# A hybrid layer on one core: four row tiles of S5's input as block products, with the first half of K split over two passes

## The chip, the core and the metric

One core of a Trainium2 chip runs one launch that computes one layer. The metric is device time in microseconds (us); less is better. The engines are called by the profile's names: PE (matrix products), DVE and ACT (element-wise work on rows of 128 partitions), POOL (element-wise work, and the queue that issues most DMAs here), SP (a queue that only issues DMAs).

## The reference, cut to what matters

The layer takes 1032 tokens: 1024 of a prompt and one for each of eight decode streams. The width is 2048.

```
h = rmsnorm(x, g_pre)
q, k, v, za, ub, zb, ga, gb = split(h @ w_in)      # 80 row tiles of 128 columns
ya = groupnorm(retention(q, k, v)) * silu(za)
yb = glu(gelu(s5(ub))) ; yb = yb * silu(zb)
y  = sigmoid(ga) * (ya @ w_pa) + sigmoid(gb) * (yb @ w_pb)
out = x + rmsnorm(y @ w_out, g_post)
```

`ub` is the input of S5, 1024 columns of `w_in`: row tiles 32 to 39 of the transposed product. S5 is a linear recurrence over tokens for each group of 16 columns, so it needs all eight tiles before it can begin. The states of both recurrences are outputs too.

## The kernel before, in words

**Number form.** Everything is float32. A product of float32 matrices is made of three matmuls on split operands: high weight by high input, high weight by low input, low weight by high input. The high part is a cast by ACT (`hi`, tiles `whia`, `whib`, `whic` in turn), the low part is the remainder that DVE subtracts (`lo`, tiles `wloa`, `wlob`, `wloc`). Weights come from memory as quarters of a row tile (128 x 512) and are split on the core; three pairs of buffers go round.

**Two ways to make a row tile of h @ w_in.** In the linear way (`linear`, L255, matmuls in `three`, L227 to L229), a row tile is four quarters of K, each with three thirds of the tokens (384, 384 and 264 columns), 16 k-tiles in all. In the other way, a pair of row tiles and half of K make a *step*: the blocks are multiplied by Winograd's form of Strassen's rule, seven products of 24 matmuls each (`product`, L923, its matmuls L935) in place of eight. The seven input operands of a half of K are 28 *form tiles* (128 x 516): sums and differences of blocks of the normed input. They are built once (`build_forms`, L767), written to the memory array `fm_d`, and later loaded, split and kept on the core. A pair is visited twice, once for each half of K. In the first visit the four results of a step are written to `pt_d` (L984); in the second they are read from it with an accumulating DMA (L986) into the tile with the new results, and go on to what the pair is for (`result`, from L978).

**The order of the work.** (1) In the start block, 16 k-tiles of `x` are loaded, scaled by `g_pre`, split, and squared for the norm, and row tiles 32 and 33 are made on the way. (2) Row tile 34 is made by `linear`; meanwhile `rms_bcast` (L278) turns the sums of squares into `rstd`, the inverse root for each token, and spreads it over 128 partitions by eight small matmuls with a diagonal matrix (L306) and one for the last 8 tokens. (3) Row tiles 35 to 39 are made by `linear` (L802, L803). Meanwhile `build_forms` makes all 56 form tiles: eight groups, each of two loads of `x` (`fx`, POOL's queue, L774), two scalings on DVE (L783), four sums or differences on DVE (`fo`, L85) and seven writes on ACT's queue (L793). (4) Two row tiles of v (16 and 17) are made by the linear way; `first_forms` meanwhile loads and splits the 28 form tiles of the first half of K. (5) 70 steps follow: 35 pairs with the first half, then 35 pairs with the second. Between the two, from two steps before the end of the first pass on, the 28 tiles on the core are replaced one by one (the *exchange*). S5 runs behind the first pass, from step 1 (`s5_params`) and step 4 (`s5_all`) on; retention behind the second. (6) Steps of the same kind for the later matrices, and the last norm.

**What sets the order.** Row tiles 32 to 39 are evacuated by `evac_ub`: DVE multiplies by `rstd` and permutes the tokens into a tile `ubp` (128 x 8 x 144: 8 runs of 128 tokens, with 8 columns of neighbours or zeros on both sides), one DMA writes it to `ub_d`, and S5 reads `U` from there. Side work is a list of generators `bg`. `slot()` (L172) advances the first of them by one `yield`; `linear` calls it once per quarter, a step once per product. What a product leaves to do later goes into `at(g, f)`, with g counted in products: `late_work(g)` runs it, and `LAG = 4` is the usual distance. Each engine works its instructions in the order in which they were written, and so does each DMA queue issue. Before a weight quarter is used, `prep` or `wtile` puts its cast into ACT's order and its remainder into DVE's, two quarters or products ahead of the matmuls.

S5 first sets the borders of a memory array `t_d` to zero: 16 times a POOL `MEMSET` of the tile `a` (L568) and a POOL DMA of it (L569). All helpers that add, subtract or multiply record their instruction at L85.

## Time and profile before

| what | value |
|---|---|
| time, median of 3 runs | 2532.88 us (2532.5 to 2534.38) |
| the profiled execution: its own time | 2534.5 us |
| its span, first to last instruction | 2532.6 us |
| instructions | 52483 |
| TensorE clock granted, mean of the span | 0.998 of full speed |
| moved by DMA | 519.10 MB, 205 GB/s in the mean |
| of it issued by POOL's queue (software) | 301.75 MB |
| third row tile of ub | 53.7 to 81.2 us |
| fourth to eighth row tile | 81.2 to 193.9 us |
| two row tiles of v | 193.9 to 239.5 us |
| 70 steps | from 239.5 us on |

The span is what the profile shows; the execution's own time is 1.9 us longer. The page gives for each engine the busy time and its share of the span; a PE that is busy can still be the bound only where nothing else ends last, which is what the chain of waits tells: it starts at the last instruction and goes back to what released it, again and again. The idle time in front of a group of instructions stands behind its busy time, with an arrow to what ended it. "x4" is the number of instructions in a group. L-numbers are those of the kernel before.

### The profile page before, as it was taken

Reading aid. Unit: us, or ns where it says so; the run is one execution under the profiler, and the core shown is the slowest. Engines: PE = TensorE matmul, PEld = TensorE weight load, DVE = VectorE, ACT = ScalarE, POOL = GpSimd, SP = SyncE. Lnnn points to the kernel's source line nnn. Section 1 sums busy time; section 2 is a strip of 40 time slices with the busy share of each in tenths; the row PEclk is TensorE's granted clock in tenths of the full one; section 3 lists DMA queues with packets and bytes.
Section 4 is the critical chain, followed back from the end, with each engine's and each line's share of the span. In section 5 each row is a group of like instructions: output and inputs, shape, how many; then the busy total and the mean of one; then the engine's idle time right before and its main releaser. Section 6 shows DMA issues by size and latency. Waiting matters only on the chain.

```text
span 2532.6 us, 52483 instructions
## 1 busy us (share of the span) xinstructions
PE 2508.4 (99%) x19948; PEld 2463.6 (97%) x19948; DVE 1975.9 (78%) x4149; ACT 965.4 (38%) x1731; POOL 763.4 (30%) x1276
## 2 busy tenths in 40 slices
PE   9999999999999999999999999999999999999998
PEld 8999999999999999999999999999999999999976
DVE  7655998898898877557986767667897878989784
ACT  7013223333333335343334444445552422455532
POOL 0103222322322222332334444434332222433320
PEclk9999999999999999999999999999999999999999
DMA  6886434444434437888879888888888689857884
GB/s 198 258 266 218 155 126 133 130 126 137 132 126 129 129 122 252 203 218 200 209 195 248 228 226 229 211 224 243 275 288 282 228 243 314 289 189 167 218 299 136
DMA packets 233755, 519.10 MB, mean 205 GB/s; under 512 B 34224, under 2 KB 61312, under 8 KB 232736
## 3 DMA queue, kind: packets, MB, share of 16 engines
q0 software_dynamic: 103008, 301.75, 41.7%
q1 hardware_dynamic: 91552, 159.30, 20.3%
q10 hardware_dynamic: 38944, 54.71, 6.8%
q8 instruction: 157, 2.57, 0.4%
q14 instruction: 94, 0.77, 0.1%
HBM read 342.37 MB, written 173.25 MB: 204 GB/s over the span
## 4 chain that ended last, share of the span: by engine, by line
PE 91%; issue 4%; DVE 2%; POOL 1%; DMA 1%; ACT 0%; POOLq 0%; DVEq 0%; SPq 0%; ACTq 0%
PE acc L935 71%; PE acc L1763 4%; PE mm L229 3%; PE mm L228 3%; PE mm L227 3%; DMA a<-mg_d 1%; DVE a L85 1%; PE misc L729 1%; PE misc L728 1%; PE misc L1134 1%; PE misc L1144 1%; PE misc L1113 1%; POOL zr L1582 1%; PE misc L679 1%; PE misc L1146 0%
## 5 line engine op out<-in xcount | busy, mean ns | idle before, releaser
L935 PE MATMUL acc<-a,whic 128*128 128x256 f32 (+1 forms) x3664 | 606.1, 284 | 1.4 <-ACT whib L916 0.6
L935 PE MATMUL acc<-a,whib 128*128 128x256 f32 (+1 forms) x3656 | 604.7, 284 | 2.5 <-DVE u L85 2.4
L935 PE MATMUL acc<-a,whia 128*128 128x256 f32 (+1 forms) x3656 | 604.7, 284 | 1.8 <-ACT whic L916 0.9
L935 PEld LDWEIGHTS acc<-a,whib 128*128 128x128 f32 x3656 | 504.4, 188 | 7.3 <-ACT whia L916 2.6
L935 PEld LDWEIGHTS acc<-a,whic 128*128 128x128 f32 x3664 | 506.2, 188 | 3.5 <-issue 1.0
L935 PEld LDWEIGHTS acc<-a,whia 128*128 128x128 f32 x3656 | 504.9, 188 | 3.9 <-issue 1.7
L935 PE MATMUL acc<-a,wloc 128*128 128x256 f32 (+2 forms) x1832 | 382.2, 283 | 0.4 <-DVE wloc L85 0.4
L935 PE MATMUL acc<-a,wlob 128*128 128x256 f32 (+2 forms) x1828 | 381.2, 283 | 0.0
L935 PE MATMUL acc<-a,wloa 128*128 128x256 f32 (+2 forms) x1828 | 381.0, 283 | 0.0
L935 PEld LDWEIGHTS acc<-a,wloc 128*128 128x128 f32 x1832 | 286.8, 188 | 1.2 <-DVE wloc L85 1.2
L935 PEld LDWEIGHTS acc<-a,wlob 128*128 128x128 f32 x1828 | 286.3, 188 | 0.2
L935 PEld LDWEIGHTS acc<-a,wloa 128*128 128x128 f32 x1828 | 286.3, 188 | 0.0
L916 ACT CAST whia<-wraw 128x512 fp32r<-128x512 f32 x142 | 88.4, 623 | 223.5 <-PE acc L935 170.4
L916 ACT CAST whib<-wraw 128x512 fp32r<-128x512 f32 x140 | 87.2, 623 | 224.7 <-PE acc L935 162.4
L916 ACT CAST whic<-wraw 128x512 fp32r<-128x512 f32 x142 | 88.4, 623 | 214.3 <-PE acc L935 155.5
L85 DVE TENSOR_TENSOR wloa<-wraw,whia 128x512 fp32r<-128x512 f32 x152 | 104.3, 686 | 58.9 <-ACT whia L916 36.0
L85 DVE TENSOR_TENSOR wlob<-wraw,whib 128x512 fp32r<-128x512 f32 x151 | 103.5, 686 | 59.1 <-ACT whib L916 39.7
L85 DVE TENSOR_TENSOR wraw<-wr 128x512 f32<-128x512 f32 x212 | 145.7, 687 | 2.7
L85 DVE TENSOR_TENSOR wloc<-wraw,whic 128x512 fp32r<-128x512 f32 x153 | 104.9, 686 | 43.5 <-ACT whic L916 28.8
L916 ACT CAST whic<-wr 128x512 fp32r<-128x512 f32 x106 | 65.9, 622 | 190.9 <-PE acc L935 157.5
L916 ACT CAST whib<-wr 128x512 fp32r<-128x512 f32 x107 | 66.6, 622 | 185.2 <-PE acc L935 154.5
L916 ACT CAST whia<-wr 128x512 fp32r<-128x512 f32 x105 | 65.3, 622 | 187.7 <-PE acc L935 153.5
(451 smaller groups left out, 4504.2 us busy)
## 6 DMA issues: line engine op xcount, KB each, us to landing
wr<-in_w_in SPq DMA_DIRECT2D x280, 256.0 KB
pt_d<-u POOLq DMA_DIRECT2D x70, 258.0 KB, 3.1
u<-pt_d POOLq DMA_DIRECT2D x70, 258.0 KB, 5.1
wr<-in_w_out SPq DMA_DIRECT2D x64, 256.0 KB
wr<-in_w_outB SPq DMA_DIRECT2D x64, 256.0 KB
stg<-fm_d POOLq DMA_DIRECT2D x44, 258.0 KB, 4.4
pt_d<-st POOLq DMA_DIRECT2D x35, 258.0 KB, 3.4
pt_d<-p POOLq DMA_DIRECT2D x35, 258.0 KB, 2.9
```

The costliest lines, as they stand in the source:

```text
L85: return (eng or V).tensor_tensor(out, a, b, op)
L227: T.matmul(ps, wh[:, i, :], xh[:, t0:t1], start=first, stop=False)
L228: T.matmul(ps, wh[:, i, :], xl[:, t0:t1], start=False, stop=False)
L229: anchor["p"] = T.matmul(ps, wl[:, i, :], xh[:, t0:t1], start=False, stop=last).ins
L679: T.matmul(ps[:, q * 144:(q + 1) * 144], W1[:, g, :], U[:, g, :], start=True, stop=True)
L728: T.matmul(o, Tm[:, g, :], U[:, g, 0:136], start=True, stop=False)
L729: T.matmul(o, W3[:, g, 1:9, :], X[:, g, 0:136], start=False, stop=True)
L916: anchor["a"] = A.copy(hi, f).ins
L935: anchor["p"] = T.matmul(o, a[:, i, :], x, start=first and i == 0 and a is wh and b is xh, stop=n in (2, 5, 6) and i == 3 and a is wl, ski ...
L1113: T.matmul(ps[:, c * 128:(c + 1) * 128], kt[:, 4 * i + c, :], vt[:, 4 * i + c, :], start=True, stop=True)
L1134: T.matmul(ps[:, c * 128:(c + 1) * 128], kT[:, cs], qT[:, cs], start=True, stop=True)
L1763: anchor["p"] = T.matmul(ps[c], a, b, start=k == 0 and a is xh and b is wh, stop=k == KD - 1 and a is xl).ins
```

## The change: what it does

Row tiles 36 to 39 are no longer made by `linear`. They become two pairs, `("ub", 36)` and `("ub", 38)`, at the head of the list of pairs, which now has 37. The first half of K is split into two passes. Pass "A" visits the first six pairs (the two of ub, three of v, the first of za) with the first half of K. Pass 0 visits all 37 pairs with the second half, beginning with the sixth pair, whose weights are of the same row tiles. Pass 1 visits pairs 6 to 36 with the first half. So there are 74 steps and two exchanges of the 28 form tiles, one before step 6 and one before step 43. Whether a visit is a pair's first is read from a list `first_visit`.

`build_forms` is called twice, for one half of K each time: for the first half under row tiles 34 and 35, with the loads of its first two groups already issued when the start block ends, and for the second half under steps 1 to 3. `linear` gets a `tick`, so that there is a slot after every third of a quarter too: 16 in a row tile where there were 4. `rms_bcast` makes the diagonal matrix of four chunks with one instruction and multiplies them with one matmul of 512 columns. The pieces of row tiles 36 to 39 reach `ub_d` by a new function `ub_rows`: four products after the accumulating read, ACT copies a half of a row tile into a permuted tile, and three POOL DMAs write it, some of them of single elements for each partition and run. S5's parameters begin at step 7 and S5 at step 10, and some later distances (`order_y`, `retention`) are counted anew.

```
+    def build_forms(kh, pool, fxs, fos, after=()):
...
+                k = 8 * kh + j + 4 * n
+                raw[k] = pool.tile([128, TOK], F32, name="fx", bufs=fxs)
+                P.dma_start(raw[k], I["xT"][k])
...
+            yield
+            for n, a, b, op in (("t1", "u1", "u2", ALU.subtract), ("t3", "u2", "v2", ALU.subtract),
+                                ("t2", "v2", "t1", ALU.add), ("t4", "v1", "t2", ALU.subtract)):
+                t[n] = pool.tile([128, HT], F32, name="fo", bufs=fos)
+                tt(t[n], t[a], t[b], op)
+                if n == "t3":
+                    yield
+            for p, n in enumerate(FORMS):
+                A.dma_start(fm_d[kh, p, j], t[n])
+            yield
+            if 1 <= j < 3:
+                load(j + 1)
+            if j < len(after):
+                after[j]()
+            yield
...
+    forms_a = build_forms(0, fb, 4, 5, (lambda: scale_ub(0), lambda: scale_ub(1)))
+    next(forms_a)
+    bg.append(first_rms())
+    bg.append(forms_a)
+    for j in (2, 3):
+        linear(w_in, M_UB + j, KD, x_of, evac_ub(j), tick=lambda kq, t: slot())
...
-    bg.append(build_forms())
-    for j in range(3, 8):
-        linear(w_in, M_UB + j, KD, x_of, evac_ub(j))
...
+            if e > i:
+                d = dg[:, 0:128 * (e - i)]
+                V.scalar_tensor_tensor(d.rearrange("p (j c) -> p j c", c=128), ident.unsqueeze(1).broadcast_to([128, e - i, 128]), float(D),
+                                       rs[:, i:e].unsqueeze(2).broadcast_to([128, e - i, 128]), ALU.mult, ALU.mult)
...
+                T.matmul(pb[:, 0:128 * (e - i)], onesk.broadcast_to([128, 128]), d, start=True, stop=True)
...
+    NP, NA = len(pairs), 6
+    B0, C0, N2 = NA, NA + NP, 2 * NP
+    HALF = {"A": 0, 0: 1, 1: 0}
+    steps = [("A", p) for p in range(NA)] + [(0, p) for p in [NA - 1] + list(range(NA - 1)) + list(range(NA, NP))] + [(1, p) for p in range(NA, NP)]
...
+    def ub_rows(dst, c, t):
+        w = ubq["pool"].tile([128, 8, 72], F32, name="ubr")
+        if c == 0:
+            P.memset(w[:, 1:8, 0:8], 0.0)
+            A.copy(w[:, :, 8:72].rearrange("p s c -> p c s"), cs(t[:, 0:512]))
+            P.dma_start(dst[:, 1:8, 0:72], w[:, 1:8])
+            P.dma_start(dst[:, 0, 8:72], w[:, 0, 8:72])
+            P.dma_start(dst[:, 0:4, 72:73], t[:, 512:516].unsqueeze(2))
+        else:
+            P.memset(w[:, 0:7, 63:71], 0.0)
+            A.copy(w[:, :, 0:63].rearrange("p s c -> p c s"), cs(t[:, 4:508]))
+            V.tensor_copy(w[:, 7, 63:71], t[:, 508:516])
+            P.dma_start(dst[:, :, 73:144], w[:, :, 0:71])
+            P.dma_start(dst[:, 4:8, 72:73], t[:, 0:4].unsqueeze(2))
+            P.dma_start(dst[:, 0, 0:8], t[:, 508:516])
...
-        if kh == 0:
+        if first_visit[s]:
             P.dma_start(pt, t)
             return
         P.dma_start(t, pt, accum_op=ALU.add)
...
+        if kind == "ub":
+            at(g + LAG, lambda: ub_rows(ub_d[(m + r - M_UB) * 128:(m + r - M_UB + 1) * 128], c, t))
+            return
...
+            change(g, B0 - 2, 0)
+            change(g, C0 - 2, 1)
```

`change` is the exchange that stood in the loop over steps before, now as a function with the step at which it begins.

Three places show how instructions move. In the first, DVE's rows of the kernel before run from the evacuation of the third row tile (`ubp<-mm,rstd`) to the first group of forms; `wloa`, `wlob` and `wloc` are the weight remainders of the fourth row tile, `fx` the scaled inputs, `fo` the forms.

```order
L85 TENSOR_TENSOR ubp<-mm,rstd 128x48x8 x2
L85 TENSOR_TENSOR ubp<-mm,rstd 128x32x8
L85 TENSOR_TENSOR ubp<-mm,rstd 128x8 x2
L783 SCALAR_TENSOR_TENSOR fx<-fx,g_pre,rstd 128x1032 x2
L85 TENSOR_TENSOR wloa<-wx_852,whia 128x512
L85 TENSOR_TENSOR fo<-fx 128x516 x2
L85 TENSOR_TENSOR fo<-fx,fo 128x516 x2
L85 TENSOR_TENSOR wlob<-wx_853,whib 128x512
L783 SCALAR_TENSOR_TENSOR fx<-fx,g_pre,rstd 128x1032 x2
L85 TENSOR_TENSOR wloc<-wraw,whic 128x512
L85 TENSOR_TENSOR fo<-fx 128x516 x2
```

The same place after the change: the first group of forms has been built by then (rows above these), and the second stands between the evacuation and the fourth tile's second quarter.

```order
L85 TENSOR_TENSOR ubp<-mm,rstd 128x48x8
L427 SCALAR_TENSOR_TENSOR fx<-fx,g_pre,rstd 128x1032
L85 TENSOR_TENSOR ubp<-mm,rstd 128x48x8
L427 SCALAR_TENSOR_TENSOR fx<-fx,g_pre,rstd 128x1032
L85 TENSOR_TENSOR ubp<-mm,rstd 128x32x8
L85 TENSOR_TENSOR ubp<-mm,rstd 128x8 x2
L85 TENSOR_TENSOR fo<-fx 128x516 x2
L85 TENSOR_TENSOR fo<-fx,fo 128x516
L85 TENSOR_TENSOR ubp<-ubp,rstd 128x8 x2
L85 TENSOR_TENSOR fo<-fx,fo 128x516
L427 SCALAR_TENSOR_TENSOR fx<-fx,g_pre,rstd 128x1032
L85 TENSOR_TENSOR wloc<-wraw,whic 128x512
```

Before, a remainder stood after every two to four instructions on forms; now seven instructions on forms (three `fx`, four `fo`) and the end of a scaling of `ubp` stand between the evacuation's first third and the one remainder.

The second place is DVE's order where a step ends and the next begins. `u`, `p` and `st` are the tiles in which results are put together out of `acc`; `wraw` are sums of weight blocks. Before, at the start of step 1 (`wr_2454` is the block of its product 0, `wraw_2641` the sum of its product 1, `wr_2460` the block of its product 2):

```order
L85 TENSOR_TENSOR wraw_2641<-wraw_2639,wr_2454 128x512
L85 TENSOR_TENSOR wraw_2737<-wr_2454,wr_2456 128x512
L85 TENSOR_TENSOR u3_2574<-u3_2574,acc_2582 128x516
L85 TENSOR_TENSOR wloa_2610<-wr_2454,whia_2609 128x512
L85 TENSOR_TENSOR p1_2438<-acc_2468,p1_2438 128x516
L85 TENSOR_TENSOR wlob_2644<-wraw_2641,whib_2643 128x512
L85 TENSOR_TENSOR u2_2493<-acc_2582,u2_2493 128x516
L85 TENSOR_TENSOR wloc_2681<-wr_2460,whic_2680 128x512
```

After, at the start of step 3 (`wr_2166` is the block of its product 0, `wraw_2358` the sum of its product 1):

```order
L85 TENSOR_TENSOR wloa_2281<-wraw_2278,whia_2280 128x512
L85 TENSOR_TENSOR u3_2272<-u3_2272,acc_2284 128x516
L85 TENSOR_TENSOR fo_2311<-fx_2209,fo_2274 128x516
L85 TENSOR_TENSOR wraw_2435<-wr_2166,wr_2168 128x512
L85 TENSOR_TENSOR fo_2313<-fx_2209,fo_2311 128x516
L85 TENSOR_TENSOR p1_2153<-acc_2180,p1_2153 128x516
L85 TENSOR_TENSOR u2_2205<-acc_2284,u2_2205 128x516
L85 TENSOR_TENSOR wlob_2323<-wr_2166,whib_2322 128x512
L85 TENSOR_TENSOR wloc_2361<-wraw_2358,whic_2360 128x512
```

The last evacuation of a step, `u2`, stood behind the remainders of the next step's products 0 and 1; now both stand behind it, because the forms `fo` were put in front.

The third place is POOL's queue while `t_d` is set to zero. Before, in steps 1 and 2, where results only are written (`pt_d<-`):

```order
L984 DMA pt_d<-st 128x516
L568 MEMSET a_3637 128x112
L569 DMA t_d<-a_3637 128x4x112
L568 MEMSET a_3637 128x112
L569 DMA t_d<-a_3637 128x4x112
L984 DMA pt_d<-u_2851 128x516
L568 MEMSET a_3637 128x112
L984 DMA pt_d<-p_2709 128x516
L569 DMA t_d<-a_3637 128x4x112
L984 DMA pt_d<-u_2768 128x516
L568 MEMSET a_3637 128x112
L569 DMA t_d<-a_3637 128x4x112
```

After, in steps 7 and 8, where `<-pt_d` are the accumulating reads and `ub_d<-` the writes of `ub_rows`:

```order
L1018 DMA u_3644<-pt_d 128x516
L1018 DMA p_3498<-pt_d 128x516
L995 DMA ub_d<-ubr 128x7x72
L996 DMA ub_d<-ubr 128x64
L1003 DMA ub_d<-u_3644 128x4x1
L1018 DMA u_3557<-pt_d 128x516
L1004 DMA ub_d<-u_3644 128x8
L997 DMA ub_d<-p_3498 128x4x1
L999 MEMSET ubr 128x7x8
L619 MEMSET a_4486 128x112
L620 DMA t_d<-a_4486 128x4x112
L1002 DMA ub_d<-ubr 1024x1x71
```

Between two zero fills stood at most two DMAs of results; now up to eight DMAs of the second visits stand there (the fill ahead of these rows is the row before the first).

More of the change, by code (lines that the diff above doesn't have):

```diff
@@ L283, in rms_bcast @@
         for i, (a, b) in enumerate(chunks):
-            T.matmul(ps[0:b - a, i:i + 1], ssq[:, a:b], onesk, start=True, stop=extra is None)
-            if extra is not None:
-                T.matmul(ps[0:b - a, i:i + 1], extra[:, a:b], onesk, start=False, stop=True)
+            T.matmul(ps[0:b - a, i:i + 1], ssq[:, a:b], onesk, start=True, stop=True)
         ms = pool.tile([128, 9], F32, name="ms")
@@ L834, in emit @@
     OUTS = ("o0", "o1")
+    first_visit = [p not in [q for _, q in steps[:s]] for s, (_, p) in enumerate(steps[:N2])]
     def otile(j):
@@ L1333, in transition, with change, load @@
                         load()
-    for s in range(2 * NP):
+    def change(g, base, kh):
+        q = g - 7 * base
+        n = moved.setdefault(kh, [0, 0])
+        def load(eng):
+            at(g, lambda o=order_q[n[0]]: stage(stg, kh, *o, eng))
+            n[0] += 1
+        if 0 <= q < 6:
+            load(nc.sync)
+            load(nc.sync)
+        if 3 <= q < 20:
+            for i in range(1 if q < 7 else 2):
+                if n[1] < 28:
+                    at(g, lambda o=order_q[n[1]]: unstage(kh, *o))
+                    n[1] += 1
+                    if n[0] < 28:
+                        load(P)
+    for s in range(N2):
         kh, p = steps[s]
```

152 lines of the change are left out of this document (68 added, 84 removed).

## The prediction

> **What bounds the kernel now.** I read the page first: the busy shares and the chain that ended last.
>
> ```profile
> PE 2508.4 (99%) x19948; PEld 2463.6 (97%) x19948; DVE 1975.9 (78%) x4149; ACT 965.4 (38%) x1731; POOL 763.4 (30%) x1276
> PE 91%; issue 4%; DVE 2%; POOL 1%; DMA 1%; ACT 0%; POOLq 0%; DVEq 0%; SPq 0%; ACTq 0%
> ```
>
> PE is busy 2508.4 of 2532.6 us and is 91% of the chain. Fewer matmul columns are therefore time saved one for one, as long as nothing that feeds PE comes late. Next I cut the span into stretches: the third row tile (53.7 to 81.2), five more row tiles, the two v rows, and the stretch in which the forms are exchanged today (920 to 1000). The columns are length, busy time of PE, weight loads, DVE, ACT and POOL, granted clock, DMA share and GB/s.
>
> ```profile
> 53.70:81.20 27.50, 27.50 (x184) 26.77 (x183) 11.06 (x29) 4.42 (x8) 4.05 (x4) 1.00 0.26 77
> 81.20:103.70 22.50, 22.50 (x145) 22.50 (x144) 16.19 (x26) 2.51 (x5) 3.79 (x12) 1.00 1.01 348
> 103.70:126.20 22.50, 22.50 (x146) 22.50 (x145) 15.07 (x22) 2.47 (x4) 2.85 (x7) 1.00 1.05 313
> 193.90:239.50 45.60, 45.01 (x288) 44.80 (x287) 20.77 (x36) 13.93 (x26) 14.68 (x29) 1.00 0.70 236
> 920.00:942.00 22.00, 22.00 (x189) 22.00 (x188) 16.02 (x31) 7.21 (x14) 6.84 (x13) 1.00 0.47 138
> 942.00:1000.00 58.00, 58.00 (x495) 58.00 (x494) 41.24 (x65) 26.01 (x46) 15.69 (x29) 1.00 0.72 234
> ```
>
> Two things are to be seen. PE has no idle time in any of these, not even where 28 form tiles are exchanged (920 to 1000). And while the forms are built (81.2 to 126.2) the DMA engines are already full: share 1.01 to 1.05 at 313 to 348 GB/s, with about two of the eight groups of forms per row tile.
>
> **What goes and what comes on PE.** Four row tiles of S5's input leave the linear form. The length of one is the distance of two evacuations that PE released (columns: start, busy, engine, line, operation, then the idle time before and its releaser):
>
> ```profile
> 171.34 0.67 DVE L85 TENSOR_TENSOR ubp<-mm,rstd 128x256 f32<-128x256 f32 x3 [0.39 <-PE mm L229]
> 193.88 0.67 DVE L85 TENSOR_TENSOR ubp<-mm,rstd 128x256 f32<-128x256 f32 x3 [0.62 <-PE mm L229]
> ```
>
> 193.88 - 171.34 = 22.54 us, so four are 90.2 us. In their place come two pairs, each visited twice: four more steps of 7 products with 24 matmuls. The chain has a stretch of 20 steps without a break:
>
> ```profile
> 941.92 395.39 PE acc L935 x3360
> ```
>
> 395.39 / 20 = 19.77 us a step (2.82 a product, 0.118 a matmul), so four are 79.1 us. **Gain on PE: 11.1 us.** That is the size of the whole change, 0.44%; 0.2% (5.1 us) is about what a measurement of this kernel can tell from none.
>
> The norm's broadcast is also rewritten. These rows are its matmuls in the third row tile:
>
> ```profile
> L306 PE MATMUL misc<-st,onesk 128*128 128x128 f32 x16 | 2.6, 287 | 0.0
> L284 PE MATMUL misc<-onesk,ssq 128*128 128x1 f32 x16 | 1.8, 245 | 0.0
> ```
>
> The row sums (1.8 us) stay. The eight 128-column matmuls (16 passes, 2.6 us) become two of 512 columns. No row shows such a one; if it costs what one of 128 does, two are 0.65, if it goes by columns, 2.6. So 0 to 2 us are saved; I take 0.8, towards the columns.
>
> **The front: three engines share a shorter cover.** Today eight groups of forms are built under five row tiles (112.7 us). Now four groups are built under the third and fourth row tile, from when rstd is there. DVE's durations for this:
>
> ```profile
> L783 DVE SCALAR_TENSOR_TENSOR fx<-fx,g_pre,rstd 128x1032 f32<-128x1032 f32 x16 | 20.3, 1288 | 3.3 <-DMA fx<-in_xT 3.2
> L85 DVE TENSOR_TENSOR fo<-fx,fo 128x516 f32<-128x516 f32 x16 | 11.1, 694 | 1.2 <-DMA fm_d<-fo 0.9
> L85 DVE TENSOR_TENSOR fo<-fx 128x516 f32<-128x516 f32 x16 | 10.5, 690 | 0.8 <-DMA fm_d<-fo 0.8
> L85 DVE TENSOR_TENSOR ubp<-mm,rstd 128x384 f32<-128x384 f32 x12 | 9.7, 833 | 2.1 <-PE mm L229 2.1
> L85 DVE TENSOR_TENSOR ubp<-mm,rstd 128x256 f32<-128x256 f32 x6 | 3.7, 616 | 1.4 <-PE mm L229 1.4
> L85 DVE TENSOR_TENSOR wloa<-wraw,whia 128x512 fp32r<-128x512 f32 x8 | 5.5, 691 | 19.1 <-ACT whia L220 16.6 <-ACT whia L916 2.5
> L85 DVE TENSOR_TENSOR ubp<-ubp,rstd 128x1024 f32<-128x1024 f32 x2 | 4.0, 1976 | 0.0
> L308 DVE COPY rstd<-misc 128x512 f32<-128x512 f32 x2 | 1.4, 692 | 0.0
> ```
>
> The critical row is wloc, the weight remainder for the fourth row tile's second quarter: in the order shown above it stands behind the third tile's evacuation, six form operations and an fx. When does DVE reach it? The third tile starts at 53.7; two quarters of 22.54 / 4 = 5.6 us, the row sums and one broadcast later (about 67.6) PE frees the hi buffer, ACT casts (0.6) and DVE makes a remainder (0.7): 68.9. From there to wloc's end stand five fx of 1.29, eight fo of 0.69, two scalings of 1.98, evacuations of 0.83, 0.83 and 0.62, one rstd copy of 0.69, eight small ones (1.3 together) and wloc itself: 21 us, less some 2 for the overlap of queued instructions, so it ends at about 88. PE needs it after two more quarters, the second broadcast, one quarter of the fourth tile and two matmuls: 85.8. **PE stalls about 2 us** without any wait for a DMA.
>
> Then there are such waits. Five buffers hold the fo forms, so the second group's last three wait for writes of the first. Today's second group shows how long those take when the DMA engines are full (a row with ACTq is the issue on ACT's queue):
>
> ```profile
> 87.94 2.37 ACTq L793 DMA_DIRECT2D fm_d<-fo  x4
> 97.73 0.70 DVE L85 TENSOR_TENSOR fo<-fx 128x516 f32<-128x516 f32 x1 [0.82 <-DMA fm_d<-fo]
> 100.07 0.69 DVE L85 TENSOR_TENSOR fo<-fx,fo 128x516 f32<-128x516 f32 x1 [0.86 <-DMA fm_d<-fo]
> ```
>
> Issued from 87.94 on, released at 97.7 and later: 10 us. In the changed kernel the first group's fo are issued from 77.4 and asked for at 84, so the wait is 0 (if the engines are less full by then) to 3.3 us; I take 1. **Stall at the fourth tile: 3 us, bounds 0 and 5.3.**
>
> The same wait decides once more, at the first v row, where wloc stands behind the fourth group's fx and three of its fo. From 74.5 on, up to there, move 19 form writes (258 KB each), four fx loads, three ub tiles and six weight quarters.
>
> ```profile
> fx<-in_xT POOLq DMA_DIRECT2D x16, 516.0 KB, 8.1
> fm_d<-fo ACTq DMA_DIRECT2D x32, 258.0 KB
> ub_d<-ubp POOLq DMA_DIRECT2D x8, 576.0 KB, 6.3
> ```
>
> That is 5.0 + 2.1 + 1.8 + 1.6 = 10.5 MB, at 348 GB/s 30 us: 104.5, and 2.5 us of DVE to wloc's end, 107. PE wants it at 85.8 + 16.9 + the 3 of above = 105.7. Stall 1 us; 0 if the traffic thins, 8.5 if it goes as in the third rival.
>
> [...]
>
> **The four steps and the second exchange.** During steps 1 to 3 the other four groups are built (now slots of 2.82 us), so DVE has a group's 2 x 1.29 + 4 x 0.69 = 5.3 us per four products, and per product about 1.5 us of weights and evacuations: 11.3 of 11.3 us. One place in the order shows it: at the start of step 3 the remainder for product 0 stands right behind the evacuation of the product before, where elsewhere it is at least one product ahead.
>
> ```profile
> L85 DVE TENSOR_TENSOR u<-acc,u 128x516 f32<-128x516 f32 (+1 forms) x100 | 67.3, 673 | 51.6 <-PE acc L935 51.3
> ```
>
> 0.67 + 0.69, less four matmuls that need no remainder (0.47): PE stalls 0.9 us; I take 1, bounds 0 and 4.4. The second exchange of 28 tiles I cost at nothing, by the rows of 920 to 1000: ACT and DVE do it there under full PE.
>
> In steps 6 to 9 POOL's queue holds more than before: accumulating reads of the second visits, the pieces of ub_rows, and among them the 16 zero fills of t_d, each waiting for the one before.
>
> ```profile
> 238.97 0.19 POOL L568 MEMSET a<- 128x112 f32 x1 [6.75 <-PE misc L229]
> 298.26 0.19 POOL L568 MEMSET a<- 128x112 f32 x1 [2.11 <-DMA t_d<-a]
> t_d<-a POOLq DMA_DIRECT2D x16, 224.0 KB, 2.8
> u<-pt_d POOLq DMA_DIRECT2D x70, 258.0 KB, 5.1
> ```
>
> The fills took 59.3 us for 15 intervals, 4.0 each, mostly waiting. Behind POOL wait ACT's copies of ub_rows, which are due four products (11.3 us) after an evacuation, and behind these the hi casts, which run two products ahead. With 5.1 us for the read, POOL may come some 6 us late before ACT waits, and 4 more before PE does. I take 0.8 us, bounds 0 and 7.
>
> **Sum:** -11.1 - 0.8 + 3 + 1 + 1 + 0.8 = -6.1 us. The profiled execution took 2534.5 us (span 2532.6), 1.6 above the median of the runs, 2532.9: so 2528.4 for such an execution, and **2526.8 us** for the median. With the bounds of its terms this case alone reaches from 2523 to 2530.5.
>
> **Rivals.**
> 1. All of it is covered: DVE catches up, since ACT and DVE work two quarters ahead in the front today without a stall (PE idle 0 in the rows above). Against it is DVE's count. -11.9 us: 2521.0.
> 2. POOL's queue decides: if a zero fill takes the 4.0 us of today's intervals instead of the 2.8 of its landing, the reads of steps 7 and 8 fall behind by about 1 us a fill; the '21' result of step 8 is then read so late that ACT holds the hi casts past both products of cover. I get some 7 us of PE for that, in place of 0.8: 2533.0, no change. For it: 12 waits on landings stand between these reads. Against it: POOL is busy only 30%. [...]
> 3. Slower: DMA engines stay full. If every form write holds its buffer for 10 us and every load takes 8.1, the third group's second fx lands near 98, the fourth's near 105, and the first v row's wloc is ready at 114 instead of 105.7: 8.5 us, with 5.3 before it. In steps 1 to 3 then 7.4 MB of forms, 4.2 of loads, 2.4 of weights and 2.4 of partials need 16.4 MB / 330 GB/s = 49.7 us where 45.3 are there: 4.4 more. -11.9 + 5.3 + 8.5 + 4.4 + 0.8 = +7.1: 2540. It decides from a write time of about 7 us on. Against it: the first two pairs of fx are now loaded early, in a stretch with DMA share 0.26.
>
> **How the numbers follow.** Chances: the forecast 0.45, full cover 0.25, POOL 0.17, DMA 0.13. The forecast's own range crosses the 0.2% mark at 2527.8; a little over half of it lies below. Faster: 0.25 + 0.27 = 0.52; same: 0.18 + 0.16 = 0.34; slower: 0.14. The range reaches from full cover (with the broadcast's 2 us bound, 2519.8) to just short of the third rival: 2520 to 2538.5.
>
> **What would show it.** Right: PE waits for "DVE wloc" of 1 to 4 us near 86 and near 105, of about 1 us at the start of step 3, a first product step near 152 to 155 instead of 239.5, nothing at the exchanges. The first rival: none of these waits. The second: ACT idle for u, p or st from pt_d in steps 7 to 9 with PE waiting for ACT casts. The third: fm_d and fx waits of 5 us and more on DVE between 85 and 115. Wrong altogether: PE idle later than step 12, or four steps that are not 19.8 us.

## The result, and the profile after

The changed kernel takes 2568.69 us (median of 4 runs, 2566.73 to 2570.47) where the kernel before takes 2533.63 in the same session: a ratio of 1.0138, 95% interval 1.012 to 1.0155. That is 35 us slower; 6 us faster was forecast, and the range ended at 2538.5. The profiled execution has a span of 2568.7 us, 36.1 more than before.

The first and the fourth part of the page, busy time and the chain of waits by engine:

```profile
PE 2531.8 (99%) x20026; PEld 2481.5 (97%) x20026; DVE 2013.5 (78%) x4200; ACT 998.3 (39%) x1787; POOL 797.4 (31%) x1328
PE 84%; issue 4%; DMA 3%; POOL 2%; DVE 2%; ACT 0%; POOLq 0%; ACTq 0%; DVEq 0%
```

Two things happened. PE's share of the chain fell from 91% to 84%: there are new waits, and PE's idle time grew from 24.2 us (2532.6 - 2508.4) to 36.9. And PE's busy time, which had to fall by 11, rose by 23.4 us. The second is the larger one, and a list of waits can't show it.

The span in stretches (columns as in the prediction: length, PE, weight loads, DVE, ACT, POOL, granted clock, DMA share, GB/s). The third row tile ends at 81.2 as before, the first product begins at 154.9:

```profile
53.70:81.20 27.50, 27.50 (x175) 26.23 (x174) 16.79 (x29) 5.28 (x10) 3.35 (x4) 1.00 0.48 168
81.20:104.00 22.80, 19.82 (x120) 19.18 (x119) 12.14 (x21) 1.24 (x2) 2.87 (x7) 0.97 1.01 349
104.00:155.00 51.00, 50.30 (x316) 49.80 (x315) 28.08 (x47) 15.88 (x28) 14.41 (x27) 0.98 0.83 285
216.00:297.00 81.00, 80.68 (x674) 80.47 (x674) 64.03 (x101) 38.12 (x67) 22.72 (x45) 1.00 0.80 258
297.00:380.00 83.00, 72.40 (x579) 71.32 (x579) 66.00 (x261) 28.48 (x45) 49.65 (x78) 0.97 0.77 176
984.00:1340.00 356.00, 356.00 (x2977) 356.00 (x2976) 269.67 (x434) 137.14 (x230) 97.79 (x151) 1.00 0.72 197
```

The front loses 3.0 us of PE's time in the fourth row tile, steps 3 to 6 next to nothing (216 to 297), and the stretch from 297 to 380, steps 7 to 10, loses 10.6. The last row holds the second exchange and the steps around it: PE is never idle there, so nothing is waited for. Yet it does 2977 matmuls in 356 us, 0.1196 each, where 0.1177 was counted on (395.39 / 3360). The chain of the changed kernel says the same, early and late:

```profile
154.92 60.59 PE acc L950 x504
1000.04 347.57 PE acc L950 x2904
```

347.57 / 2904 = 0.1197 us: a step of 168 matmuls takes 20.11 us instead of 19.77. The first three steps are no better (60.59 / 504 = 0.1202), so old steps and new are slower alike.

The two waits in the front, in PE's timeline (start, busy, then the idle time before and its releaser):

```profile
88.04 0.44 PE L229 MATMUL mm<-a,wloc 128*128 128x384 f32 x1 [0.80 <-DVE wloc L85]
...
101.76 0.45 PE L229 MATMUL mm<-a,wlob 128*128 128x384 f32 x1 [2.19 <-DVE wlob L85]
```

**A stall can cost more than its length.** Up to its last 6 us, the granted clock of the changed kernel falls to half three times, at 102.60, 331.29 and 379.08 us, for 3.41 us each. The distances, 228.69 and 47.79 us, are 67 and 14 times 3.413 us. In the trace of the kernel before it falls at 2188.71 and 2526.63 us, 99 times 3.413 us apart. So in each of the two traces the falls lie on a grid of 3.413 us. The columns of the stretches again, cut by this grid, around the stall at the fourth row tile, the first stall in step 8 and the second one, in step 9:

```profile
99.18:102.60 3.42, 1.23 (x8) 0.91 (x7) 2.79 (x4) 0.00 (x0) 0.00 (x0) 1.00 0.87 344
102.60:106.01 3.41, 3.41 (x12) 3.41 (x11) 3.38 (x5) 0.62 (x1) 0.00 (x0) 0.50 0.94 351
106.01:109.42 3.41, 3.41 (x25) 3.41 (x25) 3.08 (x6) 0.00 (x0) 0.00 (x0) 1.00 0.55 203
...
324.46:327.88 3.42, 1.56 (x14) 1.35 (x12) 2.44 (x12) 0.98 (x2) 1.80 (x3) 1.00 0.94 157
327.88:331.29 3.41, 1.42 (x12) 1.42 (x13) 3.41 (x11) 2.59 (x5) 3.10 (x7) 1.00 0.80 171
331.29:334.70 3.41, 3.41 (x18) 3.41 (x17) 3.09 (x16) 1.03 (x2) 2.54 (x4) 0.50 0.97 203
...
358.60:362.01 3.41, 1.79 (x15) 1.83 (x16) 3.31 (x15) 0.55 (x2) 3.41 (x7) 1.00 0.95 232
362.01:365.42 3.41, 3.41 (x29) 3.32 (x29) 3.24 (x19) 0.62 (x1) 1.94 (x3) 1.00 0.85 158
```

PE resumes at full clock, and the half clock comes with the next stretch of the grid: 12 matmuls in 3.41 us, where 25 follow at full clock. At half the clock for 3.41 us, that is 1.7 us more for each of these stalls. In these rows it goes by how much PE idled within one stretch of the grid: 2.19 us (3.42 - 1.23) and 1.99 us were followed by the half clock; 1.86 and 1.62 us were not. So the stall of 2.7 us in step 9, which the grid cuts in two, cost only its length. The other stretches at full clock in the traces of the two kernels, from 11 us on, agree: 3.12 us of idling (from 375.66) and 3.41 (from 2560.20) in the changed kernel, 2.33 (from 2185.30) and 3.41 (from 2523.22) in the one before were followed by the half clock, 1.76 us (from 2556.78) and 1.56 (from 2519.81) were not, and all others have less. Between 1.86 and 1.99 us these traces hold no case. In terms of single stalls it can't be told: in the changed kernel, one of 2.19 us was followed by the half clock and one of 2.71 us was not.

### The profile page after: what moved, and what is told of

Same layout as the page of the kernel before. It is cut to its first block, busy times and chain, and to the rows that moved or that the text cites. A ratio compares the mean times of both kernels' runs of the same rounds, so it can differ in the third digit from the quotient of the medians.

```text
span 2568.7 us, 52926 instructions
## 1 busy us (share of the span) xinstructions
PE 2531.8 (99%) x20026; PEld 2481.5 (97%) x20026; DVE 2013.5 (78%) x4200; ACT 998.3 (39%) x1787; POOL 797.4 (31%) x1328
## 4 chain that ended last, share of the span: by engine, by line
PE 84%; issue 4%; DMA 3%; POOL 2%; DVE 2%; ACT 0%; POOLq 0%; ACTq 0%; DVEq 0%
PE acc L950 72%; PE acc L1815 5%; PE misc L780 1%; PE misc L779 1%; PE misc L730 1%; PE misc L1169 1%; PE misc L1179 1%; PE misc L1148 1%; POOL zr L1634 1%; PE misc L1181 0%; DMA st<-pt_d 0%; PE mm L227 0%; PE mm L229 0%; PE mm L228 0%; DVE a L85 0%
## 5 line engine op out<-in xcount | busy, mean ns | idle before, releaser
L950 PE MATMUL acc<-a,whic 128*128 128x256 f32 (+1 forms) x3808 | 635.8, 286 | 5.8 <-DVE u L85 5.1
L950 PE MATMUL acc<-a,whia 128*128 128x256 f32 (+1 forms) x3800 | 634.5, 286 | 7.1 <-DVE u L85 6.6
L950 PE MATMUL acc<-a,whib 128*128 128x256 f32 (+1 forms) x3816 | 636.0, 286 | 2.4 <-DVE u L85 1.7
L950 PEld LDWEIGHTS acc<-a,whia 128*128 128x128 f32 x3800 | 533.1, 189 | 12.3 <-issue 5.7
L950 PEld LDWEIGHTS acc<-a,whic 128*128 128x128 f32 x3808 | 534.3, 189 | 8.6 <-DVE u L85 4.0
L950 PEld LDWEIGHTS acc<-a,whib 128*128 128x128 f32 x3816 | 535.0, 189 | 4.2 <-ACT whia L931 2.7
L950 PE MATMUL acc<-a,wloc 128*128 128x256 f32 (+1 forms) x1904 | 400.6, 285 | 0.5 <-DVE wloc L85 0.4
L950 PE MATMUL acc<-a,wlob 128*128 128x256 f32 (+1 forms) x1908 | 400.6, 285 | 0.5 <-DVE wlob L85 0.5
L950 PE MATMUL acc<-a,wloa 128*128 128x256 f32 (+1 forms) x1900 | 399.2, 285 | 0.0
L85 DVE TENSOR_TENSOR a<-stg,a 128x516 fp32r<-128x516 f32 (+1 forms) x224 | 136.8, 641 | 13.8 <-ACT a L274 13.4
```

Of the source, the lines that this page charges most:

```text
L85: return (eng or V).tensor_tensor(out, a, b, op)
L950: anchor["p"] = T.matmul(o, a[:, i, :], x, start=first and i == 0 and a is wh and b is xh, stop=n in (2, 5, 6) and i == 3 and a is wl, ski ...
```

## The experiments

**Where the matmul's 1.7% comes from.** The change gives the operand tiles new names, in a line that neither the account of the change nor the prediction mentions:

```
-    xs = [act.tile([128, 2, TOK], F32R, name=f"a{k}") for k in range(KD)]
+    xs = [act.tile([128, 2, TOK], F32R, name=f"a{(k + 2) % KD}") for k in range(KD)]
```

So `a0` is no longer the first tile that is placed, `a2` is. The weights' place in their buffer is chosen by the tile's number (L201). In the memory maps of the two built programs (address in a partition, in bytes):

```
              a0      a2      a4     whia    whib    whic
before     40960   57472   73984    38784   34432   36608
after     156544   40960   57472    38784   34432   36608
```

A tile is 8256 bytes long, so the first of each pair of tiles moved by 128 modulo 256 (`a0` from 0 to 128, `a2` from 128 to 0), while the 0 or 128 bytes that are added to the weights' start still went by the number. Before, the high weights and the first operand tile of a product began at the same address modulo 256; after, 128 apart. (Within a product the operands of the single matmuls begin 0 to 112 bytes further on, modulo 256, and the low weights lie 32 bytes beside the high ones. The distances given here are those of the first matmul, modulo 256: without that, in the kernel before they are even multiples of 256 bytes for 69 of the products from 942 to 1337 us and odd ones for 69 others, and both kinds take 2.824 us in the mean. After, they are 128 more than an even multiple for 64 of the products from 1000 to 1340 us, with 2.873 us, and than an odd one for 53 others, with 2.872.) Theory 1 says that this makes the matmuls slower, theory 2 that traffic or clock does.

The changed kernel with the old relation:

```
-        o = 16 if j is None else 32 * ((1 + j // 2 + (n == 2)) % 2)
+        o = 16 if j is None else 32 * ((j // 2 + (n == 2)) % 2)
```

> The changed kernel, with one number turned: the 128-byte offset at which a product's weights lie in their buffer is taken for the other parity of the operand tile, so that weights and operand tile lie to each other (address modulo 256) as in the kernel before. Theory 1 (the matmuls became slower because the tiles were renamed and weights and operands changed their relative position): the 17136 matmuls of the steps go back from 0.1197 to 0.1177 us, 34 us in all: about 2534 us. The stall of 10 us in steps 7 to 9 stays. Theory 2 (the matmuls are slower because of more DMA traffic or work on DVE beside them, or because of the clock): no change, about 2568 us.

Measured: 2549.21 us (ratio 1.0061, 1.0048 to 1.0073), 19.5 less than the changed kernel. PE's busy time on the page, 25.5 us less than in the changed kernel:

```profile
PE 2506.3 (98%) x20026; PEld 2455.6 (96%) x20026; DVE 2011.9 (79%) x4200; ACT 997.9 (39%) x1787; POOL 797.4 (31%) x1328
```

And the stretch of before, by its row:

```profile
984.00:1340.00 356.00, 354.51 (x3013) 354.33 (x3013) 272.64 (x440) 139.52 (x233) 101.75 (x157) 1.00 0.75 202
```

354.51 / 3013 = 0.1177 us: the old matmul is back, under the same traffic (202 GB/s, 197 in the changed kernel). Less came off than the 34 us that were expected. This run's own stalls are 4 us longer (1.7 in the front, 2.6 in steps 7 to 10), and the steps with S5's or retention's matmuls between gained about 1% and not 1.7%: from 1340 to 1760 PE, hardly idle in either, does 3633 matmuls where the changed kernel does 3597. Now the reverse, the same line turned in the kernel before:

> The kernel before, with the same number turned: weights and operand tile now lie to each other as in the changed kernel. Nothing else differs, no work is added. Theory 1: 16464 matmuls take 0.0020 us more, 33 us: about 2566 us. Theory 2: no change, 2533 us.

Measured: 2560.28 us, ratio 1.0098 (1.0085 to 1.0112), 25 us slower without one instruction more (33 were expected). Its chain over the same 20 steps:

```profile
948.65 402.14 PE acc L935 x3360
```

402.14 / 3360 = 0.1197, as in the changed kernel. Theory 2 falls: traffic and clock stayed (205 GB/s from 942 to 1340 us where the kernel before has 211, clock 1.00 in both), and the time moved both ways with one number. Two more kernels ask what in the place it is. In the first, every product's weights lie 64 bytes from where they did (`o = 16`), so 64 or 192 from the first operand:

> The kernel before with the weights of every product at an offset of 64 bytes, so that they lie neither as before (0 modulo 256 to the operand) nor as in the changed kernel (128) but 64 or 192 from it. Theory 1a (only the distance of 128 is bad): the step stays at 19.77 us, 2533 to 2535 us. Theory 1b (it goes by the distance): a step in between, 19.85 to 20.1 us, 2540 to 2555 us. Theory 1c (any distance but 0 costs the same): 20.11 us, 2560 us.

In the second, only the high parts move:

```
+                for p_, x, q in ((wph, "whi", o if j is None else 32 - o), (wpl, "wlo", o))]
```

> The kernel before, where the high parts of the weights alone move by 128 bytes and the low parts stay. Theory 1d (each matmul pays for the place of its own weights, two thirds of the matmuls read the high parts): a step of 20.0 us, 2550 to 2553 us, two thirds of the 25 us. Theory 1e (the low parts, which DVE writes and PE reads for one third, do it all): 19.77 to 19.88 us, 2535 to 2543 us. Theory 1f (the high parts do it all): 20.11 us, 2558 to 2561 us.

Measured: 2548.92 us (1.0058, 1.0046 to 1.0071) and 2547.72 us (1.0051, 1.0039 to 1.0063). Their chains, the 64 bytes first:

```profile
945.59 399.80 PE acc L935 x3360
```

```profile
945.15 399.19 PE acc L935 x3360
```

Steps of 19.99 and 19.96 us. The first is the step in between that theory 1b asked for. But it doesn't show that the time of a single matmul goes by its distance: with the weights at 64, half of the operands begin 0 to 112 bytes behind their high weights, modulo 256, as in the kernel before, and half 128 to 240, as in the changed one. If each matmul were either fast or slow, about half of the 0.34 us would be lost; measured are 0.22. No run separates the two. The high parts alone, read by two matmuls of three, make 56% of the 0.34 us (theory 1d asked for two thirds, and its 2550 to 2553 us were missed by 2). What makes it so, no run here shows; measured is that with the place of the weights a step changes by 1.7% (20.11 against 19.77 us).

**Where steps 7 to 10 lose 17 us.** A measure that can be read off one row: in 103 us of full work the kernel before does 878 matmuls, S5's small ones included:

```profile
300.00:403.00 103.00, 103.00 (x878) 102.20 (x878) 92.91 (x287) 32.47 (x57) 25.82 (x46) 1.00 0.41 132
```

The changed kernel, and it with the weights moved, from 297 to 400:

```profile
297.00:400.00 103.00, 92.40 (x738) 91.32 (x738) 82.90 (x313) 33.29 (x53) 55.65 (x86) 0.97 0.75 172
```

```profile
297.00:400.00 103.00, 91.18 (x729) 90.08 (x728) 82.35 (x312) 33.82 (x53) 55.11 (x85) 0.95 0.76 168
```

729 matmuls are worth 85.5 us: 17.5 are lost, 11.8 idle and the rest at half clock. (Of the changed kernel's 16.4, 1.5 belong to the slower matmul.) Here is how it begins in the changed kernel, in the timelines of POOL, ACT, DVE and PE:

```profile
301.96 0.77 POOL L620 DMA_DIRECT2D t_d<-a  x1 [0.30 <-POOL a L619]
...
308.65 0.19 POOL L619 MEMSET a<- 128x112 f32 x1 [5.37 <-DMA t_d<-a]
...
313.15 0.92 POOL L1018 DMA_DIRECT2D st<-pt_d  x1
```

```profile
319.64 1.21 ACT L994 COPY ubr<-st 128x512 f32<-128x512 f32 x1 [5.35 <-DMA st<-pt_d]
```

```profile
321.04 0.26 DVE L85 TENSOR_TENSOR ar<-mag,sc 128x96 f32<-128x96 f32 x1 [4.23 <-ACT sc L517]
...
326.90 0.17 DVE L1001 COPY ubr<-u 128x8 f32<-128x8 f32 x1 [0.98 <-DMA u<-pt_d]
```

```profile
329.87 0.39 PE L950 MATMUL acc<-a,whia 128*128 128x256 f32 x1 [3.85 <-DVE u L85]
```

A fill of `t_d` waits 5.4 us for the landing of the one before; the read `st<-pt_d` is issued behind it, ACT waits 5.35 us for the read, with weight casts and a piece of S5's set-up (`sc`) behind the copy. DVE waits 4.2 us for `sc`, and a little later itself for a read, in its own small copy of `ub_rows`. PE stands until DVE, late by then, has evacuated a product. As far as ACT's wait this is the second rival's chain; the last link is another, for it had PE waiting for ACT's casts, and all three of PE's waits from 297 to 380 (10.4 us) end with a `u` on DVE. But is the first link its cause? Eight kernels took one link or two away, all on top of the moved weights but the first (code shortened):

```
- one zero tile:     P.memset(zz, 0.0)          + if b == 0: P.memset(zz, 0.0)
- writes on SP:      P.dma_start in ub_rows     + nc.sync.dma_start
- longer lag:        at(g + LAG, ub_rows ...)   + at(g + 7, ub_rows ...)
- S5 later:          steps B0 + 1 and B0 + 4    + B0 + 3 and B0 + 6
- plain ub_rows:     memset, copy, three DMAs   + two P.dma_start of t into dst
```

One zero tile in the changed kernel, and with the weights moved:

> The changed kernel, with the zero tile of the 16 fills of t_d set to zero once instead of before each fill, so that no fill waits for the landing of the one before. Theory P (the waits on the fills' landings hold POOL's queue, and with it the reads of the second visits): most of the 10.4 us that PE waits in steps 7 to 9 go, 2558 to 2560 us, and the matmul stays at 0.1197. Rival R (the reads' own landing of 5 us, on which ACT's and DVE's copies for ub_d wait in order, is enough): less than 4 us go, 2565 to 2569 us.

> Both edits at once in the changed kernel. Theories 1 and P: 34 and about 9 us less than the changed kernel, 2525 us, so 8 us under the kernel before. With theory 1 and rival R: 2532 us. With theory 2 and P: 2559 us.

The writes on SP's queue, the longer lag, and S5 two steps later:

> The changed kernel with the weights moved as in the first experiment (2549 us there), and with the three DMAs of ub_rows issued on SP's queue in place of POOL's. Theory Q (what holds the reads of the second visits is POOL's queue with ub_rows' own writes in it, which wait for the landing of the read before): the 17 us lost in steps 7 to 9 shrink to 5 or less, 2535 to 2539 us. Rival A (ACT's copy for ub_d, four products behind the read, waits for the read's landing wherever the writes are issued): at most 5 us less, 2544 us or more. SP's weight loads now stand behind these writes; if that costs, PE waits for wr.

> The changed kernel with the weights moved, and with ub_rows seven products behind the accumulating read in place of four. Rival A (ACT waits in order for the read's landing): with 8.6 us more time the read has landed, and most of the 17 us lost in steps 7 to 9 goes, 2534 to 2540 us. Theory Q: the writes come later but stand in the same queue ahead of later reads, so ACT's copies wait as long; less than 5 us go, 2544 us or more.

> The changed kernel with the weights moved, with S5's parameters at step 9 instead of 7 and S5 at step 12 instead of 10; the fills of t_d stay where they are in POOL's queue. Theory S (S5's set-up and its small DVE work meet the second visits of ub; apart from each other they are covered): the 17 us lost in steps 7 to 10 go to 5 or less, 2536 to 2539 us. Theory T (the fills and the second visits alone are too much for POOL's queue): the losses of steps 8 and 9, some 10 us, stay, and only those at S5's start move or go: 2543 to 2549 us.

S5 later and one zero tile together:

> As the run before, and the zero tile set once, so that the 16 fills are issued one behind the other ahead of most of the second visits. Theory T: the losses go to 5 us or less, 2536 to 2539 us. Rival A (reads and ACT's copies alone suffice for the loss): no better than the run before by more than 2 us.

Then `ub_rows` as two plain DMAs, alone and with one zero tile (both leave out the permutation and the zeros, so S5 works on other numbers):

> The changed kernel with the weights moved (2549 us), where ub_rows is two plain DMAs of the result tile: the permutation of the tokens, ACT's copy, the zeros and the single elements are left out, so S5 works on other numbers. Theory U (the form of ub_rows, ACT's copy in order before the weight casts above all, makes the loss of 17 us in steps 7 to 10): 5 us or less are lost, 2535 to 2538 us. Theory V (the fills of t_d, the reads and S5's set-up lose as much without it): 2545 us or more.

> As the run before, and the zero tile of the fills set once. Theory U: the same as the run before within 2 us. Theory V: 5 us or more less than the run before, because the fills no longer hold POOL.

| on top of the moved weights | us | ratio to before, interval | matmuls in 297 to 400 |
|---|---|---|---|
| nothing | 2549.21 | 1.0061, 1.0048 to 1.0073 | 729 |
| (one zero tile, weights not moved) | 2573.74 | 1.0153, 1.0139 to 1.0167 | 744 |
| one zero tile | 2550.47 | 1.0060, 1.0046 to 1.0074 | 745 |
| writes on SP | 2546.99 | 1.0049, 1.0036 to 1.0062 | 745 |
| lag 7 | 2556.81 | 1.0089, 1.0075 to 1.0103 | 660 |
| S5 later | 2551.46 | 1.0070, 1.0058 to 1.0082 | 751 |
| plain ub_rows | 2548.68 | 1.0060, 1.0046 to 1.0073 | 749 |
| S5 later, one zero tile | 2543.14 | 1.0032, 1.0021 to 1.0044 | 791 |
| plain ub_rows, one zero tile | 2543.62 | 1.0033, 1.0020 to 1.0046 | 820 |

(With S5 later, S5 itself begins only after 400 us, so there, and with all edits below, the count of matmuls leaves its start out; the times hold it.) Alone, no edit brings more than 2.2 us, which the intervals don't tell from nothing, and theories P, Q, S and U as they were put have all failed. Rival A met its number with the writes on SP, but failed with the longer lag and with S5 later and one zero tile. (The longer lag isn't a clean test: there ACT also waits 17.1 us for the buffers of its own copies.) Theory V held in both its runs, in the second only just (5.1 us where 5 were asked for), theory T in sign only (2543 us where 2536 to 2539 were expected). Why plain `ub_rows` alone gains nothing is seen in its waits (waiting instruction, releaser, us in all, times, longest):

```profile
DVE a L624 <- DMA bc<-in_bc: 14.5, 1, 14.5
...
POOL a L619 <- DMA t_d<-a: 13.4, 9, 4.6
...
PE acc L950 <- DVE u L85: 13.1, 1, 13.1
```

The stalls of steps 8 and 9 are gone, and one of 13 us has come in their place at step 10: DVE has an instruction of S5's set-up at its head that waits for `bc`, whose load stands on POOL behind the fills and the reads, and the evacuations stand behind it. With lag 7 it is the same wait, 15.7 us. So POOL's queue runs late as a whole, and whoever comes last on it holds DVE or ACT: first the copies of `ub_rows`, without them S5's set-up. Only two links away together free a good part of it (791 and 820 matmuls, and 5 to 8 us less than the edits they are made of, with intervals that at most touch). These pairs show that the queue's waits make at least these 5 to 8 us of the loss; how much each DMA on it makes, and what makes the rest, is not settled.

**Where the front loses 6 us.** The first product begins at 154.9, where four row tiles less would give 149.4 (239.52 - 90.16). DVE waits for the load of `fx`, in the changed kernel's timelines of POOL and DVE:

```profile
78.31 0.59 POOL L418 DMA_DIRECT2D fx<-in_xT  x1 [15.69 <-DVE fo L85]
...
88.37 0.15 POOL L337 MEMSET ubp<- 128x56 f32 x1 [8.51 <-DMA ub_d<-ubp]
...
89.40 0.54 POOL L418 DMA_DIRECT2D fx<-in_xT  x1
```

```profile
99.81 1.29 DVE L427 SCALAR_TENSOR_TENSOR fx<-fx,g_pre,rstd 128x1032 f32<-128x1032 f32 x1 [10.62 <-DMA fx<-in_xT]
```

The zero fill of a new `ubp`, 8.5 us of waiting, stands ahead of the load, and the load itself, issued at 89.40, takes another 10.4 us to land. Two kernels take the load from behind it: SP's queue for the loads, and no new `ubp` (the fourth tile takes the first's).

> The changed kernel with the weights moved, and with the x loads of the third and fourth group of forms issued on SP's queue in place of POOL's, where a zero fill of a new ubp waits 8.5 us for a landing ahead of them. Theory F (the 10.6 us that DVE waits for fx, and with it PE's 2.2 to 3.8 us and the half clock behind it, come from that order on POOL): the first product begins 3 to 5 us earlier than 156.6, so 2544 to 2546 us. Rival D (the DMA engines are full there, share 1.01, and the load lands late from any queue): the first product not before 155.6, 2548 to 2549 us.

> The changed kernel with the weights moved (2549 us), where the fourth row tile's ubp takes the first one's tile with the zeros that stand in it, so that POOL has no zero fill that waits 8.5 us for a landing ahead of the x loads. Theory F (DVE's 10.6 us of waiting for fx, PE's 2.2 to 3.8 us of idling and the half clock behind it come from that wait): the second load of the third group is issued some 4 us earlier, and the first product begins at 152 to 154 us instead of 156.6: 2544 to 2546 us. Rival D (the DMA engines are full, the load lands at the same time): not before 155.6, 2548 to 2549 us.

Measured: 2555.32 (1.0086, 1.0072 to 1.01) and 2551.48 us (1.0064, 1.0052 to 1.0076), none better than 2549.21. On SP the weights' loads now stand behind loads of `x` that wait 19.0 us for their buffers (from 70 to 120 us), and PE waits 12.7 us for a `wloc` (first product at 164.7). Without the fill, POOL waits at the same place for something else:

```profile
90.03 0.54 POOL L421 DMA_DIRECT2D fx<-in_xT  x1 [5.64 <-DMA fm_d<-fx]
```

The load needs the buffer of the first group, and the writes of that group's forms land at 90. Theory F failed: the fill hid a second wait that ends at the same time. Rival D was right that the first product would not begin before 155.6 (it begins at 157.0). Last, the kernel with all edits (weights, one `ubp` less, S5 later, one zero tile, writes on SP), and the same with the third group's scalings of `x` twelve slots later, so that the weight remainders stand ahead of them, and the last group's loads issued with the third's:

> Weights moved, one ubp less, S5 two steps later, one zero tile, and ub_rows' writes on SP's queue. If each theory that names POOL's order is right, what is left is the 11 us of PE less some 5 for half clocks and rests: 2525 to 2532 us, under the kernel before. If the losses of steps 7 to 10 come from elsewhere, 2540 us or more.

> The kernel with all edits (2540 us), where the third group's scalings of x are issued twelve slots later, so that the weight remainders of the fourth row tile stand ahead of them on DVE, and the last group's loads are issued with the third's. Theory W (PE's idling at the fourth row tile comes from DVE's order alone: an instruction that waits for fx ahead of a remainder that could have been made): PE does not wait for wlob there, no half clock follows, and the first product begins at 152 to 154 us instead of 156.2: 2535 to 2538 us. Rival: the wait moves on to the first row tile of v, the first product at 155.5 or later, 2539 us or more.

All edits take 2539.82 us (1.0018, 1.0009 to 1.0026), with 835 matmuls from 297 to 400. It is the best of the changed kernels and still 4.5 us behind the one before; the expected 2525 to 2532 was missed. Its first product begins at 156.2, 6.8 us behind the 149.4, and 835 matmuls mean 5.0 us lost in steps 7 to 10. These two use up the 11.1 us that were to be gained; where the other 4.5 us go is open. The other takes 2544.35 us (1.0035, 1.0023 to 1.0047), with the first product at 158.7. In its front PE no longer waits for `wlob`, but once for a cast:

```profile
110.09 0.69 PE L227 MATMUL mm<-a,whic 128*128 128x384 f32 x1 [6.83 <-ACT whic L220]
```

On ACT's queue the cast, at 109.42, stands behind the form writes of 91.78 to 109.3 us, which wait for those same scalings. The wait moved to the first row tile of v, as the rival said. No kernel here was faster than the one before.

## Why the prediction was wrong

By its own steps:

- **PE, -11.1.** The count of steps and tiles was right, and with the weights moved back a matmul takes 0.1177 us again (984 to 1340). The step that failed is "395.39 / 20 = 19.77 us a step, so four are 79.1 us", and with it the silent premise that the other steps stay as they are. A step became 20.11 us where PE does nothing else, and slower throughout, because the tiles' new names moved operands against weights: +25 us, by the reverse experiment (2560.28 against 2534.85). The line with the names appears nowhere in the working. It was no rival, so the range could not hold it: even with every other term at its upper bound (5.3, 8.5, 4.4 and 7, and nothing from the broadcast) the sum is 2532.9 - 11.1 + 25.2 = 2547. (So the 2523 to 2530.5 that the prediction gives for its own case are not what its bounds add up to.) One of its signs of being wrong altogether, "four steps that are not 19.8 us", came true.
- **The norm's broadcast, -0.8.** Right within 0.2. The group in the changed kernel, between 53 and 104 us:

```profile
L314 PE MATMUL misc<-st,onesk 128*128 128x512 f32 x4 | 2.0, 592 | 0.0
```

  Two matmuls of two passes each are 2.0 us, where the 16 passes were 2.6: here it goes by columns, nearly.
- **The front, +4.** Near in size, in part by luck. DVE's count was right: `wloc` was ready at 88, as worked out. PE asked for it at 87.2 and not at 85.8, so the stall was 0.8 us and not 2. The wait near 105, at the first row tile of v, didn't come; instead PE waited 2.2 us for `wlob` at 101.8, because DVE waited 10.6 for a load. The first product begins at 154.9, in the range of 152 to 155 that was given. The half clock behind the longer wait (1.7 us) was not in the sum, and the wait for form writes had been priced at 0 to 3.3 us.
- **Start of step 3, +1.** PE's waits between 200 and 297 us (us in all, times, longest):

```profile
PE acc L950 <- DVE wlob L85: 0.3, 1, 0.3
```

  Right in place, a little high.
- **The second exchange, 0.** Right: no wait of PE in 984 to 1340.
- **POOL in steps 6 to 9, +0.8 (0 to 7).** The second step that failed, and the largest wait of the changed kernel: some 15 us. The second rival named its place and most of its chain (fills, reads, ACT's copies), with a chance of 0.17 and 7 us. Its last link, PE waiting for ACT's casts, was wrong: PE waited for evacuations on DVE, where S5's set-up waits for ACT and, through `bc`, for POOL's queue. The prediction did not follow that, nor the half clock behind two of the three stalls. "POOL is busy only 30%" was the wrong evidence: from 297 to 380 us POOL works for 49.7 of the 83 us and waits 29.0 for landings.
- **The third rival** (DMA engines full). Its sign came, a wait of DVE for `fx` of over 5 us between 85 and 115, and the load landed at 99.8 where it said 98. Its price, 8.5 us at the first v row, did not: what that wait cost PE was the 2.2 us and the half clock behind it.

Together: -11.1, about 6 in the front (5.5, from 149.4 to 154.9 us), 15 in steps 7 to 10 (the 16.4 without the slower matmul's 1.5) and 25 in the matmuls make +35, against the span's 36.1.

## What to carry to other kernels

Where PE bounds a kernel at 99%, ask of every edit whether it moves a buffer. Here the tiles' new names cost 25 us where the work that was saved was worth 11.1, and it showed as more time for the same number of matmuls in a stretch without idle time, not as a wait. Look at a queue that issues DMAs where the edit works, and not at the mean of the span: POOL, busy 31% of the span, was late in steps 7 to 10, where it waits 29.0 of 83 us for landings. Follow all who are served by it; here two links had to go together before 5 to 8 us came free, since without the first wait the next one showed (14.5 us for `bc`, with the plain `ub_rows`). And look at the granted clock behind a stall of PE: three stalls of the changed kernel had a phase of 0.50 behind them, 1.7 us each.

## What the runs showed of the hardware that was not expected

With the place of the weights against the moving operand the matmul's time changed. Counted by the addresses in a partition modulo 256 bytes, and in the kernel before with nothing else changed, it is 0.1177 us in the mean when the high weights and the first operand of a product begin at the same place (395.39 / 3360), 0.1190 with 64 or 192 bytes between them (399.80 / 3360, `f3_before_weights_at_64`) and 0.1197 with 128 (402.14 / 3360, `e2_before_weights_moved`). These are means over matmuls whose operands begin up to 112 bytes further on; the law for a single matmul stays open, and so does the cause.

PE's granted clock fell, in the traces of the kernels `before` and `after`, at distances that are whole multiples of 3.413 us (67, 14 and 99). A stretch of this grid at full clock in which PE idled 1.99 us or more was followed by one at 0.50 in all six cases, a stretch with 1.86 us or less never. These are counts of two traces, not a rule.
